# V of a pair of heads stored as head, 64 zeros, head: the products of attention weights and V over 128 columns

## The chip, the cores and the metric

The kernel runs on one core of a Trainium2 chip. Its time is the device time of one execution in microseconds (us); lower is better.

## What is computed

Two layers over a sequence of 512 tokens of width 1024, in fp32: a layer of stick-breaking attention with 16 heads of 64, a layer of a gated linear recurrence (HGRN2), each followed by a squared-ReLU MLP of width 4096. The change lies in the attention:

```python
for t0 in range(0, seq, 128):
    t1 = t0 + 128
    z = einsum('bhqd,bhkd->bhqk', q[:, :, t0:t1], k[:, :, :t1]) * scale
    causal = arange(t1)[None, :] < (t0 + arange(128))[:, None]
    log_stay = where(causal, log_sigmoid(-z), 0.0)
    log_between = cumsum(log_stay, axis=3, reverse=True) - log_stay
    weights = where(causal, exp(log_sigmoid(z) + log_between), 0.0)
    outs.append(einsum('bhqk,bhkd->bhqd', weights, v[:, :, :t1]))
```

The output of the heads goes through a projection (`sb_w_o`) and is added to the residual stream.

## The kernel before

The tokens are four blocks of 128 (`TT = 4`). Matrix products with weights run as three fp32r matmuls per step, on a high and a low part of each operand: the weights come as slabs of 256 or 512 columns, each in two halves of 512 KB. SyncE fetches a half into a raw buffer (tag `wr`, three buffers, line 257), ScalarE casts it to the high part (`wh`, line 266), VectorE subtracts to get the low part (`wl`, line 267). High and low parts have two buffers each, so the slab ahead is split as soon as TensorE has left the slab before. The first slab is written into two `wr` buffers by hand (line 1170) and split in four pieces at lines 540 and 541.

Attention (`attention`, line 501) goes over four groups of four heads. For a group it projects Q, K and V (`gemm_x`, 24 matmuls of 256 columns per block of tokens) and starts tasks for its two pairs of heads. `prepare_pair` (line 615) transposes K and Q of a pair (`pk`, `pq`). `head` (line 642) is one head: `z_of(T)` makes the scores of token block T and their sigmoids (`sn`, `sg`, lines 661 and 662), a scan and a product on VectorE (lines 664 and 668); `turn(T)` transposes the weights of block T, T + 1 transposes into `pa`, and brings them to SBUF as `at` (lines 682 and 683); `apply(T)` multiplies them with V:

```python
o = blk(shared["po"], T)[j * SB_DH : (j + 1) * SB_DH, :]
for b in range(T + 1):
    mm(o, vs[0][:, b, hc : hc + SB_DH], blk(at[T], b), b == 0, b == T)
```

V is the stationary operand (128 tokens by the 64 columns of one head), the weights are the moving one (128 columns), all fp32. Head j = 0 of a pair writes partitions 0 to 63 of the bank `po`, head j = 1 partitions 64 to 127. Per head these are 1 + 2 + 3 + 4 = 10 matmuls, 160 in all; the trace shows an fp32 matmul that is no transpose as two rows. When both heads are done, `split_out` (line 416) brings the bank to SBUF as `oh` and `ol`.

The order of TensorE's work is fixed by hand: `Line` counts an estimated time for each matmul and takes up the tasks by the delays in `LAG`, between the matmuls of the projections. So the pieces of a head stand among projection matmuls, and a run of `po` matmuls is followed by projections, by scores or by transposes. The order of the other engines' work is set by the scheduler of the language from priorities and its own estimate.

The tag `B` (two buffers) holds V of a group, later a part of the MLP's raw weights and V of the recurrence; line 607 writes V, scaled, on ScalarE. In the MLP a round is four slabs of `mlp_w1` (lines 844 to 862), and then seven half slabs made from `mlp_w2` (`Seven`), whose raw parts (`raw`, line 288) are fetched on the same queue of SyncE. Four rounds make one MLP, and there are two MLPs.

Of the kernel before, what the change touches and what calls it, by code (L numbers as in the profile page):

```python
# [8 lines left out]
F32 = mybir.dt.float32  # L9
# [3 lines left out]
AF = mybir.ActivationFunctionType  # L13
# [3 lines left out]
P = 128  # L17
D = 1024
S = 512
KT = D // P  # L20
TT = S // P
EPS = 1e-6
SLAB = 256
FF = 4 * D
SB_DH = 64
# [34 lines left out]
def trunk(  # L60
# [17 lines left out]
    nc = tc.nc  # L78
    PSUM = bass.MemoryType.PSUM
    cp = ctx.enter_context(tc.tile_pool(name="cp", bufs=1))  # L80
    wp = ctx.enter_context(tc.tile_pool(name="wp", bufs=2))
# [10 lines left out]
    def sb(tag, shape=(P, S), dt=F32, name=None):  # L92
        pool = gp if tag in "PQ" else ap
        return pool.tile(list(shape), dt, tag=tag, bufs=BUFS[tag], name=name or tag)
# [57 lines left out]
    def mm(o, lhsT, rhs, start, stop, **kw):  # L152
        n = rhs.shape[-1]
        nc.tensor.matmul(o, lhsT=lhsT, rhs=rhs, start=start, stop=stop, **kw)  # L154
        line.at += COST[rhs.dtype] * max(n, 64)
# [5 lines left out]
    def blk(t, n):  # L161
        return t[:, n * P : (n + 1) * P]
# [16 lines left out]
    def gain(layer, j, kt):  # L179
# [15 lines left out]
        out=later[:, 3 * P :], in_=later[:, 3 * P :], pattern=[[-1, P]], compare_op=ALU.is_gt,  # L195
# [4 lines left out]
        out=before[:, P:], in_=before[:, P:], pattern=[[1, P]], compare_op=ALU.is_gt,  # L200
# [49 lines left out]
    def slab_halves(spec):  # L250
        w, r0, kt, c0, nc_ = spec
        hi = wp.tile([P, kt, nc_], F32R, tag="wh", bufs=2, name="wh")
        lo = wp.tile([P, kt, nc_], F32R, tag="wl", bufs=2, name="wl")
        h = kt // 2

        def load(a):
            raw = wp.tile([P, h, nc_], F32, tag="wr", bufs=3, name="wr")
            r = r0 + a * h * P
            nc.sync.dma_start(
                out=raw, in_=w[r : r + h * P, c0 : c0 + nc_].rearrange("(k p) c -> p k c", p=P)  # L260
            )
            return raw

        def split(a, raw):
            c = slice(a * h, (a + 1) * h)
            nc.scalar.copy(hi[:, c, :], raw)  # L266
            nc.vector.tensor_tensor(out=lo[:, c, :], in0=raw, in1=f(hi[:, c, :]), op=ALU.subtract)  # L267

        return hi, lo, load, split

    def seven(w, r0):

        b = {}

        def rows(i, j, a):
            r = r0 + i * (D // 2) + a * 2 * P
            return w[r : r + 2 * P, j * S : (j + 1) * S].rearrange("(k p) c -> p k c", p=P)

        def load(i, j):

            tag = {(0, 0): "B", (1, 0): "X5", (0, 1): "R4", (1, 1): "R4"}[i, j]
            shape = (P, 10 * P) if tag == "X5" else (P, TT, SLAB)
            b[i, j] = []
            for a in range(2):
                t = sb(tag, shape, name="raw")
                t = t if tag == "X5" else t.rearrange("p t c -> p (t c)")
                t = t[:, : 2 * S].rearrange("p (k c) -> p k c", c=S)
                nc.sync.dma_start(out=t, in_=rows(i, j, a))
                b[i, j].append(t)

        def flip(at, plus):

            for a in range(2):
                nc.scalar.mul(b[at][a], b[at][a], -1.0)  # L294
                nc.gpsimd.dma_start(out=b[at][a], in_=plus(a), accum_op=ALU.add)

        def slab(at):
            hi = wp.tile([P, KT // 2, S], F32R, tag="wh", bufs=2, name="wh")
            lo = wp.tile([P, KT // 2, S], F32R, tag="wl", bufs=2, name="wl")
            for a in range(2):  # L300
                c = slice(2 * a, 2 * a + 2)
                nc.scalar.copy(hi[:, c, :], b[at][a])  # L302
                nc.vector.tensor_tensor(  # L303
                    out=lo[:, c, :], in0=b[at][a], in1=f(hi[:, c, :]), op=ALU.subtract
                )
            return hi, lo

        def early():
            load(0, 1)
            load(1, 1)  # L310

        def t1():
            flip((0, 1), lambda a: rows(0, 0, a))

        def slab_t1():
            got = slab((0, 1))
            for a in range(2):
                nc.gpsimd.dma_start(out=b[0, 1][a], in_=rows(1, 1, a), accum_op=ALU.add)  # L318
            flip((0, 0), lambda a: b[0, 1][a])
            return got  # L320

        def slab_b21():
            got = slab((1, 0))
            flip((1, 0), lambda a: b[0, 1][a])
            return got

        slabs = [
            lambda: slab((0, 0)), slab_t1, slab_b21, lambda: slab((1, 1)), lambda: slab((0, 1)),
            lambda: slab((0, 0)), lambda: slab((1, 0)),
        ]  # L330
        steps = (early, lambda: load(0, 0), lambda: load(1, 0), t1)
        return [("load", g) for g in steps], [("slab", g) for g in slabs]
# [168 lines left out]
    def attention(norm):  # L501
# [23 lines left out]
        wsl, raws = start["w"], start["raws"]  # L525
# [38 lines left out]
        for g in range(4):  # L564
            ss = sb("ss", (P, 2, 4 * TT), name="ss") if g else ss0
            qk = [] if g else [dst]
            for which in range(len(qk), 2):
                dst = sb("R4", (P, TT, SLAB), name="qk")
                qk.append(dst)
                wsl = weights.next()  # L570
                for hf in range(2):
                    p = ps("mm" if g else "tr")
                    for u in range(2):
                        yield from gemm_x(p[:, u * SLAB : (u + 1) * SLAB], wsl, 2 * hf + u, acts)
                    evac(p, 2 * hf, 2, which, dst, ss)
            m = sb("mqk", (P, 32), name="mqk")
            for which in range(2):
                nc.vector.scalar_tensor_tensor(
                    out=m[:, 16 * which : 16 * which + 16].rearrange("p (t h) -> p t h", h=4),
                    in0=ss[:, which, :].rearrange("p (t h) -> p t h", h=4), scalar=1.0 / SB_DH,  # L580
                    in1=em[:, :, None].to_broadcast([P, TT, 4]), op0=ALU.mult, op1=ALU.add,
                )
            rq = rsqrt(m, 32, "rq")
            q, k = qk
            for which in range(2):
                v = qk[which].rearrange("p t (h d) -> p (t h) d", d=SB_DH)
                nc.vector.tensor_tensor(
                    out=v, in0=v,
                    in1=rq[:, 16 * which : 16 * which + 16, None].to_broadcast([P, 16, SB_DH]),
                    op=ALU.mult,  # L590
                )
            vs = []
            for pair in range(2):
                shared = {"po": None}
                ready = line.spawn(prepare_pair(q, k, pair, shared))
                for j in range(2):
                    heads.append(line.spawn(head(ready, vs, pair, j, shared, outs, 2 * g + pair)))
            wsl = weights.next()
            V = sb("B", (P, TT, SLAB), name="V")
            for hf in range(2):  # L600
                p = ps("mm")
                for u in range(2):
                    yield from gemm_x(p[:, u * SLAB : (u + 1) * SLAB], wsl, 2 * hf + u, acts)
                for u in range(2):
                    t = 2 * hf + u
                    nc.scalar.activation(
                        out=V[:, t, :], in_=p[:, u * SLAB : (u + 1) * SLAB], func=AF.Copy,
                        scale=r[:, t : t + 1],
                    )
            vs.append(V)  # L610
        return outs, heads
# [30 lines left out]
    def head(ready, vs, pair, j, shared, outs, slot):  # L642
        yield [ready]
        yield max(0.01, shared["at"] + LAG["q"][j] - line.at)
        kst, qh, ql = shared["k"][j], shared["q"][j], shared["ql"][j]
        hc = (2 * pair + j) * SB_DH
        while live["sg"] >= BUFS["X5"]:
            yield 0.2
        live["sg"] += 1
# [35 lines left out]
        def apply(T):  # L685
            if shared["po"] is None:
                shared["po"] = ps("av", name="po")
            o = blk(shared["po"], T)[j * SB_DH : (j + 1) * SB_DH, :]
            for b in range(T + 1):
                mm(o, vs[0][:, b, hc : hc + SB_DH], blk(at[T], b), b == 0, b == T)  # L690

        for step in LAG["head"]:
            if isinstance(step, float):
                yield step
            else:
# [3 lines left out]
                {"z": z_of, "t": turn, "a": apply}[kind](T)  # L699
                if step == ("t", TT - 1):  # L700
                    live["sg"] -= 1
        if j == 1:
            outs[slot] = split_out(shared["po"])


# [173 lines left out]
    def hgrn(norm):  # L879
# [4 lines left out]
        for hp in range(4):  # L884
# [19 lines left out]
            for j in range(2):  # L904
# [14 lines left out]
                got[j] += [fr, kk]  # L919
                if j == 0:  # L920
                    task = line.spawn(take_turns(got, LAG["s0"]))
            V = sb("B", (P, TT, SLAB), name="Vh")
            G = sb("R4", (P, TT, SLAB), name="G")
            for n in range(2):
                wsl = weights.next()
# [228 lines left out]
    def trunk_steps():  # L1154
# [12 lines left out]
    w0, r0, _, c0, _ = weights.plan.pop(0)  # L1167
    start = {
        "w": [wp.tile([P, KT, SLAB], F32R, tag=t, bufs=2, name=t) for t in ("wh", "wl")],
        "raws": [wp.tile([P, KT // 2, SLAB], F32, tag="wr", bufs=3, name="wr") for _ in range(2)],  # L1170
    }
    for c in range(4):
        for j in range(2):
# [73 lines left out]
```

## Time and profile before

| | us |
|---|---|
| runs: lowest, median, highest | 1294.69, 1297.34, 1298.52 |
| the profiled execution | 1297.17 |
| its span | 1295.5 |
| TensorE busy in the span | 1259.6 (97%) |
| VectorE busy | 956.2 (74%) |
| ScalarE busy | 611.6 (47%) |
| GpSimd busy | 146.7 (11%) |

A busy time counts the time in which at least one instruction ran; matmuls overlap, so a busy TensorE need not be at its peak. For TensorE the distance between two starts says more than the length of a row. Rows of the timeline give start, length, engine, line, operation, tiles (out<-in), rows by columns of the stationary operand and shape of the moving one, and the number of merged instructions; an idle time ahead of a row stands in brackets, with what ended it.

### The profile page before, as it was taken

The numbers are of one execution on the slowest core, as the hardware profiler recorded it, in microseconds if no ns is written. First come the engines' busy times: TensorE is split into PE (matmuls) and PEld (weight loads), VectorE is DVE, ScalarE is ACT, GpSimd is POOL, SyncE is SP. The second block draws the span as 40 slices with busy tenths as digits, with TensorE's granted clock in tenths as the row PEclk, the third lists the DMA queues.
The fourth block names the chain that finished last, engine by engine and source line by source line (L and its number), as shares of the span: only waits on it lengthen the run. The fifth ranks groups of instructions, "written<-read, shape, count | busy, mean of one in ns | idle before, by whom it ended". The sixth has DMA issues, their size and how long they took to land. (4 is left out here: it accounts for less than half of the span.)

```text
span 1295.5 us, 17920 instructions
## 1 busy us (share of the span) xinstructions
PE 1259.6 (97%) x6817; PEld 1069.5 (83%) x6817; DVE 956.2 (74%) x1799; ACT 611.6 (47%) x991; POOL 146.7 (11%) x203
## 2 busy tenths in 40 slices
PE   7999999999999999999999999999999999999998
PEld 7989898778877878878878888888888788788787
DVE  4787688765676875867878888888666768667686
ACT  4555455534563634645552423333255536446362
POOL 1000001000020110100113131314000201002010
PEclk8999999999999999999999999999999999999999
DMA  6312124223285393671532222124521954827515
GB/s 185 106 33 66 34 66 130 83 89 90 66 179 178 72 237 114 125 212 54 97 98 66 65 66 72 59 85 137 170 69 62 215 164 84 246 74 172 169 31 133
DMA packets 104502, 144.23 MB, mean 111 GB/s; under 512 B 4856, under 2 KB 70560, under 8 KB 104416
## 3 DMA queue, kind: packets, MB, share of 16 engines
q1 hardware_dynamic: 91024, 109.22, 26.0%
q0 software_dynamic: 13392, 33.87, 14.8%
q8 instruction: 54, 0.88, 0.3%
q14 instruction: 32, 0.26, 0.1%
HBM read 124.19 MB, written 2.10 MB: 97 GB/s over the span
## 5 line engine op out<-in xcount | busy, mean ns | idle before, releaser
L154 PE MATMUL ps_mm<-xh,wh 128*128 128x512 f32 x592 | 232.6, 393 | 4.0 <-DVE xt L707 4.0
L154 PE MATMUL ps_mm<-xh,wl 128*128 128x512 f32 x592 | 230.5, 389 | 0.0
L154 PE MATMUL ps_mm<-xl,wh 128*128 128x512 f32 x592 | 230.5, 389 | 0.0
L266 ACT CAST wh<-wr 128x1024 fp32r<-128x1024 f32 x134 | 136.4, 1052 | 138.2 <-PE ps_mm L154 121.5
L267 DVE TENSOR_TENSOR wl<-wr,wh 128x1024 fp32r<-128x1024 f32 x134 | 163.2, 1232 | 17.1 <-ACT wh L266 17.0
L154 PE MATMUL ps_mm<-wh,xh 128*128 128x256 f32 x592 | 173.5, 293 | 0.0
L154 PE MATMUL ps_mm<-wl,xh 128*128 128x256 f32 x592 | 167.7, 283 | 2.7 <-DVE wl L541 2.7
L154 PE MATMUL ps_mm<-wh,xl 128*128 128x256 f32 x592 | 167.6, 283 | 0.0
L303 DVE TENSOR_TENSOR wl<-raw,wh 128x1024 fp32r<-128x1024 f32 x112 | 132.7, 1220 | 35.8 <-ACT wh L302 35.7
L154 PEld LDWEIGHTS ps_mm<-xh,wh 128*128 128x128 f32 x592 | 111.2, 188 | 28.7 <-issue 6.3
L302 ACT CAST wh<-raw 128x1024 fp32r<-128x1024 f32 x112 | 111.4, 1047 | 44.0 <-PE ps_mm L154 40.4
L154 PEld LDWEIGHTS ps_mm<-xh,wl 128*128 128x128 f32 x592 | 111.1, 188 | 23.3
L154 PEld LDWEIGHTS ps_mm<-xl,wh 128*128 128x128 f32 x592 | 111.2, 188 | 22.3
L707 DVE TENSOR_TENSOR xt<-xt,ps_mm 128x512 f32<-128x512 f32 x128 | 86.0, 682 | 47.9 <-PE ps_mm L154 47.7
L154 PEld LDWEIGHTS ps_mm<-wh,xh 128*128 128x128 f32 x592 | 113.4, 192 | 4.1 <-issue 3.6
L154 PEld LDWEIGHTS ps_mm<-wl,xh 128*128 128x128 f32 x592 | 113.5, 192 | 3.4 <-DVE wl L541 2.9
L154 PEld LDWEIGHTS ps_mm<-wh,xl 128*128 128x128 f32 x592 | 113.5, 192 | 0.0
L859 DVE SCALAR_TENSOR_TENSOR u<-ps_mm,R 128x512 f32<-128x512 f32 x60 | 41.4, 690 | 63.7 <-PE ps_mm L154 63.7
L318 POOL DMA_DIRECT2D raw<-in_mlp_w_dram x16 | 19.4, 1243 | 591.1 <-DVE wl L303 591.1
L294 ACT ACTIVATE raw<-raw 128x1024 f32<-128x1024 f32 x48 | 50.7, 1058 | 36.4 <-DMA raw<-in_mlp_w_dram 36.3
L664 DVE TENSOR_TENSOR_SCAN sn<-sn,later 128x128 f32<-128x128 f32 (+3 forms) x64 | 51.2, 816 | 8.1 <-ACT sn L661 7.1
L1021 DVE COPY_PREDICATED sc<-masks,ps_s 128x32 f32<-128x32 uint8 (+9 forms) x176 | 46.5, 298 | 13.0 <-PE ps_s L154 11.0
(235 smaller groups left out, 2538.9 us busy)
## 6 DMA issues: line engine op xcount, KB each, us to landing
raw<-in_mlp_w_dram SPq DMA_DIRECT2D x64, 512.0 KB, 6.3
wr<-in_mlp_w_dram SPq DMA_DIRECT2D x64, 512.0 KB, 4.5
raw<-in_mlp_w_dram POOLq DMA_DIRECT2D x32, 512.0 KB, 6.1
raw<-raw POOLq DMA_DIRECT2D x32, 512.0 KB, 6.1
wr<-in_hg_w_in_dram SPq DMA_DIRECT2D x32, 512.0 KB, 3.8
wr<-in_sb_w_qkv_dram SPq DMA_DIRECT2D x22, 512.0 KB, 3.7
wr<-in_sb_w_o_dram SPq DMA_DIRECT2D x8, 512.0 KB, 3.9
wr<-in_hg_w_o_dram SPq DMA_DIRECT2D x8, 512.0 KB, 4.0
```

What stands on the lines that cost most here:

```text
L154: nc.tensor.matmul(o, lhsT=lhsT, rhs=rhs, start=start, stop=stop, **kw)
L266: nc.scalar.copy(hi[:, c, :], raw)
L267: nc.vector.tensor_tensor(out=lo[:, c, :], in0=raw, in1=f(hi[:, c, :]), op=ALU.subtract)
L294: nc.scalar.mul(b[at][a], b[at][a], -1.0)
L302: nc.scalar.copy(hi[:, c, :], b[at][a])
L303: nc.vector.tensor_tensor(out=lo[:, c, :], in0=b[at][a], in1=f(hi[:, c, :]), op=ALU.subtract)
L318: nc.gpsimd.dma_start(out=b[0, 1][a], in_=rows(1, 1, a), accum_op=ALU.add)
L664: nc.vector.tensor_tensor_scan(out=rev, data0=rev, data1=later[:, S - W :][:, ::-1], initial=1.0, op0=ALU.mult, op1=ALU.max,)
L707: nc.vector.tensor_tensor(out=xt[h][:, t, :], in0=xt[h][:, t, :], in1=p, op=op)
L859: nc.vector.scalar_tensor_tensor(out=u, in0=p, scalar=0.0, in1=norm.R, op0=ALU.max, op1=ALU.mult)
L1021: nc.vector.copy_predicated(out=o, mask=mask.rearrange("p (g w) -> p g w", g=g)[:, None].to_broadcast([P, 2, g, w]), data=data.rearrange(" ...
```

## The change

V of a group becomes a tile of 128 x 4 x 2 x 192: for each token block and pair of heads first the 64 columns of head 0, then 64 zeros, then the 64 columns of head 1. GpSimd clears the middle (a new `memset` for each group, line 599 of the changed kernel), ScalarE writes the two heads in one instruction with a gap. The stationary operand of head 0 is columns 0 to 127 (head, zeros), that of head 1 columns 64 to 191 (zeros, head), so every product covers all 128 partitions of `po`, and both heads add into the same block; the first of the 20 matmuls of a pair starts the bank and the last one stops it. The bank is taken out by the head that comes last. V now needs half as much space again, so all users of tag `B` take tiles of 1536 elements, and the raw buffers `wr` become two instead of three.

```diff
-            raw = wp.tile([P, h, nc_], F32, tag="wr", bufs=3, name="wr")
+            raw = wp.tile([P, h, nc_], F32, tag="wr", bufs=2, name="wr")
...
-            shape = (P, 10 * P) if tag == "X5" else (P, TT, SLAB)
+            shape = (P, {"X5": 10 * P, "B": 12 * P, "R4": 8 * P}[tag])
...
-                shared = {"po": None}
+                shared = {"po": None, "n": 0}
...
-            V = sb("B", (P, TT, SLAB), name="V")
+            V = sb("B", (P, TT, 2, 3 * SB_DH), name="V")
+            nc.gpsimd.memset(V[:, :, :, SB_DH : 2 * SB_DH], 0.0)
...
+                    v = V[:, t].rearrange("p a (b d) -> p a b d", d=SB_DH)[:, :, 0::2, :]
                     nc.scalar.activation(
-                        out=V[:, t, :], in_=p[:, u * SLAB : (u + 1) * SLAB], func=AF.Copy,
-                        scale=r[:, t : t + 1],
+                        out=v, in_=p[:, u * SLAB : (u + 1) * SLAB].rearrange(
+                            "p (a b d) -> p a b d", b=2, d=SB_DH
+                        ),
+                        func=AF.Copy, scale=r[:, t : t + 1],
                     )
...
-            o = blk(shared["po"], T)[j * SB_DH : (j + 1) * SB_DH, :]
+
+            o = blk(shared["po"], T)
             for b in range(T + 1):
-                mm(o, vs[0][:, b, hc : hc + SB_DH], blk(at[T], b), b == 0, b == T)
+                shared["n"] += 1
+                mm(
+                    o, vs[0][:, b, pair, j * SB_DH : j * SB_DH + P], blk(at[T], b),
+                    shared["n"] == 1, shared["n"] == TT * (TT + 1),
+                )
...
-        if j == 1:
+        if shared["n"] == TT * (TT + 1):
             outs[slot] = split_out(shared["po"])
...
-            V = sb("B", (P, TT, SLAB), name="Vh")
+            V = sb("B", (P, 12 * P), name="Vh")[:, : 8 * P].rearrange("p (t c) -> p t c", c=SLAB)
...
-        "raws": [wp.tile([P, KT // 2, SLAB], F32, tag="wr", bufs=3, name="wr") for _ in range(2)],
+        "raws": [wp.tile([P, KT // 2, SLAB], F32, tag="wr", bufs=2, name="wr") for _ in range(2)],
```

TensorE, the second and third run of `po` of the first pair of heads, among projection matmuls (`ps_mm`) and transposes (`pa`); the numbers are columns of the output's partitions by columns moved:

```order
 L154 MATMUL ps_mm<-wh,xl 128x256
 L158 MATMUL pa<-ident,sg 128x128 x3
-L154 MATMUL po<-at,V 64x128 x2
+L154 MATMUL po<-at,V 128x128 x2
 L158 MATMUL pa<-ident,sg 128x128 x2
-L154 MATMUL po<-at,V 64x128
+L154 MATMUL po<-at,V 128x128
 L154 MATMUL ps_mm<-wh,xh 128x256
 L154 MATMUL ps_mm<-wl,xh 128x256
```

Nothing moved: on TensorE the whole program keeps its order, and only the width of the 160 products differs.

ScalarE at the start, from the last split of the first slab (line 540 before, 539 now) over the casts of the K slab (line 266) to the evacuation of the first Q projection. Before:

```order
L540 CAST wh<-wr 128x512
L266 CAST wh<-wr 128x1024 x2
L511 ACTIVATE sqq<-ps_mm 128x256
L517 COPY qk<-ps_mm 128x256
L511 ACTIVATE sqq<-ps_mm 128x256
L517 COPY qk<-ps_mm 128x256
L511 ACTIVATE sqq<-ps_z 128x256
```

Now:

```order
L539 CAST wh<-wr 128x512
L266 CAST wh<-wr 128x1024
L510 ACTIVATE sqq<-ps_mm 128x256
L516 COPY qk<-ps_mm 128x256
L510 ACTIVATE sqq<-ps_mm 128x256
L516 COPY qk<-ps_mm 128x256
L266 CAST wh<-wr 128x1024
L510 ACTIVATE sqq<-ps_z 128x256
```

The cast of the second half of the K slab went behind four evacuations.

The queue of SyncE at the border from the first to the second round of the first MLP: halves of `mlp_w1` slabs (`wr`) and the raw parts of `mlp_w2` of the round (`raw`). Before:

```order
L259 DMA wr_4073<-in_mlp_w1_dram 128x4x256
L259 DMA wr_4077<-in_mlp_w1_dram 128x4x256
L259 DMA wr_4115<-in_mlp_w1_dram 128x4x256
L288 DMA raw_4025<-in_mlp_w2_dram 128x2x512
L288 DMA raw_4027<-in_mlp_w2_dram 128x2x512
...
L288 DMA raw_4191<-in_mlp_w2_dram 128x2x512
L259 DMA wr_4119<-in_mlp_w1_dram 128x4x256
L259 DMA wr_4195<-in_mlp_w1_dram 128x4x256
```

Now:

```order
L259 DMA wr_4077<-in_mlp_w1_dram 128x4x256
L259 DMA wr_4081<-in_mlp_w1_dram 128x4x256
L287 DMA raw_4029<-in_mlp_w2_dram 128x2x512
L287 DMA raw_4031<-in_mlp_w2_dram 128x2x512
...
L287 DMA raw_4195<-in_mlp_w2_dram 128x2x512
L259 DMA wr_4119<-in_mlp_w1_dram 128x4x256
L259 DMA wr_4123<-in_mlp_w1_dram 128x4x256
L259 DMA wr_4199<-in_mlp_w1_dram 128x4x256
```

The first half of slab 1 of the next round (`wr_4115` before, `wr_4119` now) went from ahead of the eight `raw` fetches to behind them.

## Rows read from the trace of the kernel before

**Rows 1.** Attention: us, then PE, PEld, DVE, ACT, POOL busy, clock, DMA, GB/s.

```profile
47.00:290.00 243.00, 237.73 (x1695) 207.20 (x1694) 186.91 (x350) 122.33 (x260) 8.17 (x13) 0.99 0.24 73
```

**Rows 2.** TensorE's waits, 47 to 300 us: total us, times, longest.

```profile
PE z L154 <- ACT sg L662: 3.2, 3, 1.2
PE po L154 <- DVE at L683: 1.2, 2, 0.6
```

**Rows 3.** Timeline of TensorE, the first run of `po`: start, length in us.

```profile
70.69 0.38 PE L158 MATMUL pa<-ident,sg 128*128 128x128 f32 x2
71.00 0.43 PE L154 MATMUL po<-at,V 128*64 128x128 f32 x2
71.36 0.38 PE L154 MATMUL ps_mm<-wh,xh 128*128 128x256 f32 x1
71.58 0.28 PE L154 MATMUL ps_mm<-wl,xh 128*128 128x256 f32 x1
```

**Rows 4.** Timeline, VectorE and TensorE, a run between transposes.

```profile
76.80 0.59 DVE L683 TENSOR_TENSOR at<-pa,before 128x256 f32<-128x256 f32 x2
...
77.26 0.87 PE L154 MATMUL po<-at,V 128*64 128x128 f32 x6
...
78.06 0.55 PE L158 MATMUL pa<-ident,sg 128*128 128x128 f32 x3
```

**Rows 5.** Timeline of TensorE, the last run of `po`.

```profile
286.05 1.09 PE L154 MATMUL po<-at,V 128*64 128x128 f32 x8
287.07 0.50 PE L154 MATMUL ps_mm<-wh,oh 128*128 128x512 f32 x1
```

**Rows 6.** Timeline of TensorE, transposes of K and Q among projections.

```profile
59.26 0.28 PE L154 MATMUL ps_mm<-wh,xl 128*128 128x256 f32 x1
59.38 0.60 PE L158 MATMUL pk<-ident,qk 128*128 128x128 f32 x4
59.82 0.60 PE L158 MATMUL pq<-ident,qk 128*128 128x128 f32 x4
60.17 0.36 PE L154 MATMUL ps_mm<-wh,xh 128*128 128x256 f32 x1
60.38 0.28 PE L154 MATMUL ps_mm<-wl,xh 128*128 128x256 f32 x1
```

**Rows 7.** Timeline of TensorE, full-width fp32 products in the recurrence.

```profile
722.34 0.61 PE L154 MATMUL po_h<-Vh,sc 128*128 128x128 f32 x4
```

**Rows 8.** Groups of instructions by form: weight loads (busy us, mean ns).

```profile
L154 PEld LDWEIGHTS po<-at,V 128*64 128x64 f32 x320 | 33.3, 136 | 12.6 <-issue 7.1 <-DVE at L683 2.0 <-ACT sg L662 0.7
L154 PEld LDWEIGHTS po_h<-Vh,sc 128*128 128x128 f32 x64 | 9.4, 192 | 0.3
```

**Rows 9.** Timeline at the start: VectorE, the queue of SyncE, TensorE.

```profile
25.79 0.68 DVE L541 TENSOR_TENSOR wl<-wr,wh 128x512 fp32r<-128x512 f32 x1
...
26.50 0.37 SPq L259 DMA_DIRECT2D wr<-in_sb_w_qkv_dram  x1
...
31.28 0.28 PE L154 MATMUL ps_tr<-wl,xh 128*128 128x256 f32 x1
```

**Rows 10.** DMA issues: times, KB each, median us from issue to landing.

```profile
wr<-in_mlp_w_dram SPq DMA_DIRECT2D x64, 512.0 KB, 4.5
...
wr<-in_sb_w_qkv_dram SPq DMA_DIRECT2D x22, 512.0 KB, 3.7
```

**Rows 11.** Timeline of VectorE and ScalarE, border of rounds in the first MLP.

```profile
396.39 1.22 DVE L267 TENSOR_TENSOR wl<-wr,wh 128x1024 fp32r<-128x1024 f32 x1
...
398.13 1.22 DVE L267 TENSOR_TENSOR wl<-wr,wh 128x1024 fp32r<-128x1024 f32 x1
...
401.39 1.05 ACT L266 CAST wh<-wr 128x1024 fp32r<-128x1024 f32 x1 [2.57 <-DMA wr<-in_mlp_w_dram]
...
404.10 0.69 DVE L859 SCALAR_TENSOR_TENSOR u<-ps_mm,R 128x512 f32<-128x512 f32 x1 [0.40 <-PE ps_mm L154]
...
409.31 2.01 ACT L266 CAST wh<-wr 128x1024 fp32r<-128x1024 f32 x2 [3.42 <-PE ps_mm L154]
```

More of the change, by code (lines that the diff above doesn't have):

```diff
@@ L285, in load @@
                 t = sb(tag, shape, name="raw")
-                t = t if tag == "X5" else t.rearrange("p t c -> p (t c)")
                 t = t[:, : 2 * S].rearrange("p (k c) -> p k c", c=S)
@@ L645, in head @@
         kst, qh, ql = shared["k"][j], shared["q"][j], shared["ql"][j]
-        hc = (2 * pair + j) * SB_DH
         while live["sg"] >= BUFS["X5"]:
```

## The prediction

> **What bounds the kernel now.** I read the busy times by stretch first, because the change edits one stage: attention runs from about 47 to 290 us. There TensorE is busy 237.73 of 243 us, VectorE 186.91, ScalarE 122.33 and GpSimd 8.17 [rows 1]. So TensorE sets the pace of this stage, and what it no longer does is worth time, as long as VectorE (77% busy) keeps up. The list of TensorE's waits says the same from the other side: before 300 us the two largest are 3.2 us in 3 waits on the sigmoids of the scores and 1.2 us in 2 waits on the finished attention weights [rows 2]. Then I read TensorE's instructions in order of time around the products of weights and V (`po`), because busy time hides what lies between two pipelined matmuls; the number to read is the distance from one start to the next.
>
> The first run of `po` is one fp32 matmul, which the trace shows as two rows. Ahead of it stand two transposes at 70.69; they follow each other after 0.11, so the second starts at 70.80 and the first `po` row at 71.00, 0.20 later. From 71.00 to the next projection matmul are 0.36 us, and from that one to its successor 0.22 [rows 3]. In the last run eight rows need 1.02 us from the first of them to the start behind the run [rows 5]. A run between transposes takes 0.80 for six rows until the next transpose [rows 4]. Now the same kind of place without the 64-column shape: fp32 transposes over the full 128 columns. They start 0.12 after a projection matmul, follow each other at 0.11, the next projection matmul starts 0.35 after the first of four, and its successor 0.21 later [rows 6]. Three steps of 0.109 are 0.327 of that 0.35, so leaving a full-width group costs some 0.03, where leaving a `po` run costs 0.20. TensorE thus pays when it changes between the 64-column shape and the full one, at both ends of every run.
>
> **What the change does, part by part.**
>
> *The switch.* The order of TensorE's instructions stays; each of the 160 `po` matmuls becomes 128 columns wide. There are 64 runs, the first at 71.00 [rows 3], the last at 286.05 [rows 5]; 43 are followed by projections or scores and 21 by transposes. For one run that ends in projections, with its times from the rows: entering 0.20 instead of 0.11, saved 0.09; the first step inside is 0.16 instead of 0.11 (0.36 = 0.16 + 0.20 [rows 3]; 1.02 = 0.16 + 6 x 0.11 + 0.20 [rows 5]), saved 0.05; leaving 0.20 instead of 0.03, saved 0.17; the step behind it 0.22 instead of 0.21, saved 0.01. Together 0.32, times 43 is 13.8 us. For a run ahead of transposes: 0.09 + 0.05, then 0.20 to the transpose instead of 0.11, and the step after that again 0.16 instead of 0.11: 0.28, times 21 is 5.9 us. Sum 19.7. The steps inside may become a little longer: four full-width fp32 rows that are no transposes take 0.61 [rows 7] where four transposes take 0.60 [rows 6], so some 0.003 a step, 256 steps, 0.8 us. I take **19 us** off TensorE. From below, if only the way out were saved (the 43 x 0.17), it is 7 us; a loss is possible only by the weights, which is a rival below.
>
> *The wider weights.* A load of 64 columns takes 136 ns, a full-width fp32 load 192 [rows 8]. On 320 rows that is 320 x 56 ns = 17.9 us more of loading. I cost it at nothing, since loads run beside the matmul ahead: the rows of [rows 7] have 192 ns loads and still follow each other within 0.11. The Trainium skill, "TensorE: Matmul & The Clock Gate", section on LDWEIGHTS, has a load take its columns divided by 1.2 GHz, so by the page 53 ns more each and an estimate of 17 us: the rule speaks against the change, the trace has the same price but shows it covered, and by the rule alone almost all of the gain would be gone.
>
> *How much of the 19 us comes through.* The weights that `po` reads come from VectorE. The run at 77.26 starts while the two instructions that finish its weights run from 76.80 to 77.39 [rows 4]: here TensorE already stands at the edge. Three runs lie ahead of it in this burst, so about 1 us that they and its own entry save turns into a wait there. Bounds: if VectorE's work in the stage stays at 186.91 us against 243 - 19 = 224, it is 83% busy, and nothing need be lost; if in each of the eight pairs of heads one such edge takes back all that four runs save (4 x 0.31), 10 us are lost. I take half, **5 us**: the first pair of a group has its scores, transposes and weights packed close and the second has gaps.
>
> *One staging buffer less, at the start.* The raw halves of the weights now share two buffers instead of three, and the first slab holds both. So the second half of the K slab can only be fetched when the last split of the first slab ends, at 25.79 + 0.68 = 26.47; in the trace the queue issues its next fetch at 26.50 [rows 9]. It lands after 3.7 us [rows 10], at 30.2, is cast in 1.05 and split in 1.22 (durations of [rows 11]), so it is ready at 32.5. TensorE wants it for the fifth of eight steps of the K projection; that low half is first read at 31.28 [rows 9]. Cost **1.2 us**, from 0 (landing in 2.5 us) to 3. ScalarE's order is already bent round it: that cast now stands behind four evacuations.
>
> *The same buffer in the MLPs.* At the six borders between rounds the third buffer lets the first half of slab 1 arrive long ahead. Now it waits for the split that begins at 396.39 and ends at 397.61, the second half for the next, about 399.3. With a landing of 4.5 us [rows 10] the second half is there at 403.85, cast and split by 406.1, and the evacuation of the first product, which stands behind that split on VectorE, is done at 406.8 instead of 404.79. TensorE is on slab 0 until 409.31 [rows 11], and only then needs that bank and those weights. Cover 2.5 us, cost nothing; where a landing is longer than 7 us, all beyond it is paid six times. In the trace of before ScalarE waits 2.57 us at this border for the second half and nobody on TensorE notices.
>
> *The rest.* Four clears of the zero columns go to GpSimd; 13 instructions took it 8.17 us in this stage [rows 1], so some 0.6 each, on an engine that is idle for 235 us; the third clear waits for the first group's products, and behind it stand only clears for later heads. The evacuations of V write the same number of elements in two pieces. The order of ScalarE and VectorE changes by a few places within a pair (the cast of the finished pair comes ahead of two sigmoids); I cost it at nothing, plus or minus 2 us.
>
> Sum: -19 + 5 + 1.2 = **-12.8 us**. The profiled execution took 1297.17 us (1295.5 of span), which is 0.2 under the median 1297.34; so 1284.4 against that execution, and 1284.5 against the median.
>
> **The rivals.** *All comes through*: no edge takes anything back, -18, 1279. For it: few waits now, VectorE at 77%. Against it: the edge at 77.26. *Half of it comes back*: the edges take 10 us, -8, 1289.5. *No change*: the wider loads are not covered in a `po` run, because here the stationary operand is V and every row loads anew; -19 + 17.9 + 1.2 = 0, 1297. Against it [rows 7], the same fp32 shape with V in this kernel, though there V is the moving operand. It also covers the case in which the switch is not what costs the 0.20, so that the full shape keeps it. *Slower*: the two staging buffers. Place: second half of slab 1 at the six borders of rounds. To end 4 us above the median it must return the gain and more, 17 us, so 2.8 at each border: a landing of 7 + 2.8 = 9.8 us would do it, 1301.5. Against it the 4.5 us landing; for it that other transfers of the MLP run in the same stretches.
>
> **How the numbers follow.** A measurement of this kernel can tell about 0.3%, 3.9 us. Forecast with its own bounds, 0.60; all comes through, 0.12; half comes back, 0.15; no change, 0.08; slower, 0.05. The first three are faster by more than 3.9 us: 0.87. Range: down to 1276, where everything comes through and the granted clock, 0.99 in this stage [rows 1], comes to 1.00 (up to 2.4 us); up to 1292, where 10 us come back, the start costs 3 and another short fall of the clock comes in. That leaves out the two last cases.
>
> **What would show it.** Right: `po` rows of 128 columns, next projection 0.03 behind a run's last row, the first step 0.11; the attention stage 12 to 14 us shorter, with TensorE's waits on the weights and the sigmoids up by about 5. A wait of about 1 us at 31 us on the split of the K slab. Nothing at the MLP borders but a longer wait of ScalarE for the fetch. Wrong: `po` steps of 0.17 or more (the loads), a distance of 0.20 still standing behind runs (not the switch), TensorE waiting for weights at the round borders (the buffer), or VectorE above 90% in the stage.

## The result and the profile after

The changed kernel took **1283.69 us** (median of 3 runs, 1282.32 to 1284.05) against 1297.34: a ratio of 0.9890, 95% interval 0.9866 to 0.9913. That is 13.65 us less; 12.8 were forecast. On a second chip its ratio to the kernel before was 0.9912 (0.9899 to 0.9926). The profiled execution took 1282.32, its span 1280.6; against the 1295.5 of before that is 14.9 us less. Its mean granted clock is 0.996, the same as before.

Line numbers shift by a few in the changed kernel: the sigmoids are line 664, the attention weights 685, the projection's addition to the residual 714.

**The stage.** The work that stood between 47 and 290 us [rows 1] now ends 16 us earlier, so the same piece is 47 to 274 (columns as there: us, busy PE, PEld, DVE, ACT, POOL, clock, DMA share, GB/s):

```profile
47.00:274.00 227.00, 219.92 (x1696) 209.83 (x1695) 186.32 (x353) 121.43 (x260) 9.07 (x15) 0.99 0.26 79
```

TensorE has 1696 instructions as it had 1695, and VectorE 186.32 us of work as it had 186.91; only the stage is shorter. The granted clock is alike in both: 1.00 but for one short stretch at 0.50, the lower of TensorE's two levels (1.2 GHz), from 251 to 254 us before and from 240 to 243 now, each time behind two waits of about 0.9 and 1.0 us (in the second trace of the changed kernel, below, the same two waits stand with no such stretch). VectorE is now busy for 186.32 of 227 us, 82%, where the prediction had worked out 83%. Weight loads run for 209.83 us, 2.6 us more than before in a stage that is 16 us shorter; what hides them is tried below.

**The runs of `po`.** The timeline of TensorE at the first run and at the last one (start, length, us), which answer to [rows 3] and [rows 5]:

```profile
70.92 0.38 PE L158 MATMUL pa<-ident,sg 128*128 128x128 f32 x2
71.13 0.39 PE L154 MATMUL po<-at,V 128*128 128x128 f32 x2
71.28 0.36 PE L154 MATMUL ps_mm<-wh,xh 128*128 128x256 f32 x1
71.48 0.28 PE L154 MATMUL ps_mm<-wl,xh 128*128 128x256 f32 x1
...
270.38 1.05 PE L154 MATMUL po<-at,V 128*128 128x128 f32 x8
271.19 0.47 PE L154 MATMUL ps_mm<-wh,oh 128*128 128x512 f32 x1
```

From the first `po` row to the projection behind it were 0.36 us and are now 0.15: one step of 0.11 and 0.03 to leave. The eight rows of the last run took 1.02 us to the next start and now take 0.81, which is 7 x 0.11 and 0.03. From the start of the first run to the start of the last one it was 286.05 - 71.00 = 215.05 us; now it is 270.38 - 71.13 = 199.25. So **15.8 us** went between these two rows, and 0.2 more in the last run: all of the gain lies in this stage.

**What came back.** TensorE's waits from 47 to 300 us (total us, times, longest), to be read beside [rows 2]. The third of them was there before as well; its row of before comes first, then the three of now, then the run that stood at the edge in [rows 4]:

```profile
PE ps_mm L154 <- DVE xt L707: 1.0, 1, 1.0
```

```profile
PE z L154 <- ACT sg L664: 3.1, 3, 1.1
PE po L154 <- DVE at L685: 3.0, 6, 0.6
PE ps_mm L154 <- DVE xt L714: 1.0, 1, 1.0
```

```profile
77.67 0.49 PE L154 MATMUL po<-at,V 128*128 128x128 f32 x2 [0.61 <-DVE at L685]
78.00 0.49 PE L158 MATMUL pa<-ident,sg 128*128 128x128 f32 x3
```

The waits on the weights rose from 1.2 us in 2 to 3.0 in 6; the sigmoids and the one evacuation stay where they were. That is 7.1 us of idle time in place of 5.4, 1.7 more. Counted from start to start, the four runs that wait now and did not before (at 77.67, 92.09, 191.61 and 209.35 us) take 0.78, 0.33, 0.78 and 0.56 us longer at that step than before: **2.4 us** came back, where 5 were allowed.

**Outside the stage.** Three places, in the order of time: the start, a border of two rounds in the first MLP, and the border to the recurrence (first the timeline of TensorE; then of ScalarE and VectorE; then of ScalarE, with TensorE's waits from 630 to 660 us):

```profile
31.44 0.38 PE L154 MATMUL ps_tr<-wl,xh 128*128 128x256 f32 x1 [0.88 <-DVE wl L267]
```

```profile
388.15 1.05 ACT L266 CAST wh<-wr 128x1024 fp32r<-128x1024 f32 x1 [1.70 <-DMA wr<-in_mlp_w_dram]
...
390.38 0.69 DVE L866 SCALAR_TENSOR_TENSOR u<-ps_mm,R 128x512 f32<-128x512 f32 x1
...
393.34 2.01 ACT L266 CAST wh<-wr 128x1024 fp32r<-128x1024 f32 x2 [1.17 <-PE ps_mm L154]
```

```profile
637.41 1.05 ACT L266 CAST wh<-wr 128x1024 fp32r<-128x1024 f32 x1 [0.30 <-DMA wr<-in_hg_w_in_dram]
```

```profile
PE ps_x L158 <- DVE xl L435: 2.0, 2, 1.3
```

At the start TensorE waits 0.88 us for the second half of the K slab, as forecast; from start to start it falls back by 1.1 us between 30 and 48 us (from 0.9 ahead of the kernel before to 0.2 behind it). At the round border the evacuation ends at 390.38 + 0.69 = 391.07 and TensorE leaves slab 0 at 393.34, 16 us earlier than at the same place of before [rows 11]: 2.3 us to spare, and TensorE does not wait. At the border to the recurrence ScalarE's cast waits 0.30 us for a fetch, which it did not do before; the evacuations of the transposes stand behind that cast, and TensorE's wait for them is 2.0 us, where the kernel before had 1.2 in the same stretch (645 to 675 us there):

```profile
PE ps_x L158 <- DVE xl L436: 1.2, 2, 0.6
```

So 0.8 us were lost at a place that the prediction had not looked at. The price of this place is not fixed. In the second trace of the changed kernel (run again, below) TensorE waits longer there, and the granted clock then lies at the lower level, where the first trace has 1.00 (the waits from 630 to 660 us, and a stretch with the columns of the stage's row):

```profile
PE ps_x L158 <- DVE xl L435: 3.3, 2, 2.4
```

```profile
640.00:646.00 6.00, 5.06 (x16) 4.28 (x17) 4.33 (x12) 2.02 (x4) 0.00 (x0) 0.50 0.27 87
```

In that execution 3.5 us went at this border against the kernel before. From start to start, the step with the longer of the two waits is 0.98 us in the three traces with three staging buffers, and 1.5 to 2.8 us in the ten with two.

Sum over the span: -16.0 in the stage, +1.1 at the start, +0.8 at the recurrence, +0.2 in the second MLP, and -0.9 because the first transfers (blocks of `x`, the gain of K) landed that much earlier in this execution, which is chance: the row that stands at 31.16 us before stands at 32.82 and 29.75 in two experiments with the same start. That is -14.8, and the span shows -14.9.

### The profile page after: what moved, and what is told of

It reads as the page before. It is cut to its first block, busy times and chain, and to the rows that moved or that the text cites. A ratio compares the mean times of both kernels' runs of the same rounds, so it can differ in the third digit from the quotient of the medians.

```text
span 1280.6 us, 17916 instructions
## 1 busy us (share of the span) xinstructions
PE 1241.3 (97%) x6817; PEld 1071.3 (84%) x6817; DVE 955.4 (75%) x1799; ACT 611.1 (48%) x991; POOL 148.4 (12%) x207
## 3 DMA queue, kind: packets, MB, share of 16 engines
q0 software_dynamic: 13392, 33.87, 14.9%
## 5 line engine op out<-in xcount | busy, mean ns | idle before, releaser
L154 PE MATMUL ps_mm<-wl,s31h 128*128 128x512 f32 x128 | 51.2, 400 | 4.1 <-DVE wl L302 4.1
```

## The experiments

Two theories on the gain were to be told apart (the 64-column shape costs at every change of shape, or something else in the change brings the time), and one question on the loss: do the two staging buffers, or the order of VectorE, make the new waits? Each ratio below is to runs of the kernel before beside it on the same chip, with medians of 1295.58, 1295.81 or 1295.68 us; it can differ a little from the quotient of two medians. Differences in us are worked out from the ratio and 1297.34.

**The width alone.** The kernel before with 128 columns of V and nothing else: no zeros, three staging buffers.

```diff
...
-            o = blk(shared["po"], T)[j * SB_DH : (j + 1) * SB_DH, :]
+            o = blk(shared["po"], T)
...
-                mm(o, vs[0][:, b, hc : hc + SB_DH], blk(at[T], b), b == 0, b == T)
+                mm(o, vs[0][:, b, pair * P : (pair + 1) * P], blk(at[T], b), b == 0, b == T)
```

> The kernel before, in which only the width of the product changes: the stationary operand is the 128 columns of both heads of the pair as V lies before (no zeros, no memset, three staging buffers, the starts and stops of before), so the two heads overwrite each other and the output is not the reference's. Theory (the 64-column shape costs TensorE a change at both ends of every run): the whole gain and a little more, since the staging buffer stays: attention 16 us shorter, no wait at 31 us, 15.5 to 18 us under the kernel before, 1279 to 1282. Rival (the gain comes from the single accumulation of both heads, the later bank or the new order of VectorE): within 4 us of before.

Measured: 1280.78 us, ratio 0.9875 (0.9859 to 0.9890), so 16.2 us (14.3 to 18.3) below the kernel before. Its waits in the stage, 47 to 300 us:

```profile
PE z L154 <- ACT sg L661: 3.1, 3, 1.1
PE po L154 <- DVE at L682: 3.0, 6, 0.6
PE ps_mm L154 <- DVE xt L706: 1.4, 2, 1.0
```

The width carries the whole gain. (Its stage is 1.0 us shorter than the changed kernel's, but the granted clock is 1.00 all through it; the second trace of the changed kernel has 1.00 and the same length.) The waits on the weights are the same 3.0 us in 6 as in the changed kernel, with three staging buffers and the old order on ScalarE and VectorE. So they are the refill: TensorE has become faster than what feeds it. The wait at the start and the longer one at the recurrence are absent here (1.2 us in the latter stretch, as before).

**Two buffers alone.** The kernel before with `bufs=2` for `wr` in both places.

> The kernel before with two staging buffers instead of three and nothing else. Theory (what the traces of before and after show as the price of the buffer: a wait of 1.04 us at 31 us and 0.7 us more at the border from the first MLP to the recurrence): 1 to 2.5 us slower than before, about 1299. Rival A (the buffer costs at the borders of MLP rounds, hidden in the change by its gain): 4 us and more. Rival B (it costs nothing): within 0.5 us.

Measured: 1299.35 us, ratio 1.0025 (1.0016 to 1.0034), so 3.2 us more (2.1 to 4.4), between the theory and its first rival. Its timeline has both waits of the changed kernel, TensorE's at the start and ScalarE's at the recurrence:

```profile
31.08 0.39 PE L154 MATMUL ps_tr<-wl,xh 128*128 128x256 f32 x1 [0.86 <-DVE wl L267]
```

```profile
654.64 1.05 ACT L266 CAST wh<-wr 128x1024 fp32r<-128x1024 f32 x1 [0.37 <-DMA wr<-in_hg_w_in_dram]
```

From start to start they cost 1.1 and 0.8 us, and the borders of MLP rounds add nothing. Of the rest, 0.9 us stands at 385 us and 0.5 at 555, where TensorE waits for the weights made from `mlp_w2`. Whether the buffer causes these is open. At the first place the wait is 0.1 to 0.3 us in the three traces with three buffers and 0.0 to 1.1 in the ten with two; at the second it is 0.4 to 0.8 and 0.3 to 0.8. A shift of the same kind, 1.2 us, also stands in the second MLP of the width alone, which has three buffers.

**More runs, narrow and wide.** If the price is paid for each change of shape, more runs must cost, and with the full width they must not. The products of token blocks 2 and 3 (three and four matmuls) are cut into two runs, with one step of the projections between them where one is left: 92 runs in place of 64.

```diff
-            main = Task(gen)
+            main = self.main = Task(gen)
...
-        def apply(T):
+        def apply(T, blocks=None):
...
-            for b in range(T + 1):
+            for b in blocks or range(T + 1):
...
-                {"z": z_of, "t": turn, "a": apply}[kind](T)
+                if kind == "a" and T > 1:
+                    apply(T, range(2))
+                    if line.main.ready(line.at) and not line.main.done:
+                        line.main.step(line.now)
+                    apply(T, range(2, T + 1))
+                else:
+                    {"z": z_of, "t": turn, "a": apply}[kind](T)
```

In the kernel before (64 columns):

> The kernel before with the product of token blocks 2 and 3 cut in two by one step of the projection (three matmuls of 256 columns, taken from where they stood before): 92 runs of 64-column products instead of 64, the same 6817 rows of TensorE. Theory (0.33 us for each run: 0.09 in, 0.05 after the first step, 0.17 out, 0.02 behind): 28 x 0.33 = 9 us slower than before, 1305 to 1308. Rival (the cost is per product, of the 64-column shape itself, or of the first run of a burst only): within 2 us of before.

In the changed kernel (128 columns):

> The changed kernel with the same cut: 92 runs of 128-column products instead of 64. Theory (no change of shape, no price of a run): within 1.5 us of the changed kernel, 1282 to 1285. Rival (any cut between fp32 and fp32r products costs, and the width only hides it): about 9 us slower than the changed kernel, 1293.

Measured: 1306.28 us in the kernel before, ratio 1.0077 (1.0064 to 1.0091), so 10.0 us (8.3 to 11.8) for 28 more runs, **0.36 us a run** (0.30 to 0.42). In the changed kernel 1282.4 us, ratio 0.9899 (0.9885 to 0.9914) against 0.9890 without the cut: no difference. The same piece in both traces, the first two blocks of a cut product, narrow and then wide (TensorE's timeline):

```profile
75.85 0.65 PE L154 MATMUL po<-at,V 128*64 128x128 f32 x4
76.43 0.39 PE L154 MATMUL ps_mm<-wh,xh 128*128 128x256 f32 x1
76.65 0.28 PE L154 MATMUL ps_mm<-wl,xh 128*128 128x256 f32 x1
```

```profile
76.44 0.61 PE L154 MATMUL po<-at,V 128*128 128x128 f32 x4
76.81 0.36 PE L154 MATMUL ps_mm<-wh,xh 128*128 128x256 f32 x1
77.01 0.28 PE L154 MATMUL ps_mm<-wl,xh 128*128 128x256 f32 x1
```

Four narrow rows hold TensorE for 0.58 us until the projection, four wide ones for 0.37, and the entry costs its 0.09 besides. This settles that the change of shape is the cost.

**How near are the loads?** The prediction took the wider loads as covered. Here each product moves two halves of 64 columns, with a load of the same 128 columns of V for each: twice the loads, the same columns moved.

```diff
-                mm(
-                    o, vs[0][:, b, pair, j * SB_DH : j * SB_DH + P], blk(at[T], b),
-                    shared["n"] == 1, shared["n"] == TT * (TT + 1),
-                )
+                for c in range(2):
+                    u = slice(c * P // 2, (c + 1) * P // 2)
+                    mm(
+                        o[:, u], vs[0][:, b, pair, j * SB_DH : j * SB_DH + P], blk(at[T], b)[:, u],
+                        shared["n"] == 1 and c == 0, shared["n"] == TT * (TT + 1) and c == 1,
+                    )
```

> The changed kernel with each of the 160 products cut into two that move 64 columns of weights each, so 640 rows and 640 full-width weight loads instead of 320. The columns moved stay the same, only the loads double. Theory 1, the loads are only just covered by a step of 0.112 us: a row of half the moving columns still takes about 0.11, the 320 rows more cost 320 x 0.11 = 35 us, 1319 us, PE's starts inside a run 0.11 apart. Theory 2, the loads are well covered (a load costs at most half a step): rows follow at 0.056, time as the changed kernel, 1284 plus or minus 3. In between, the distance inside a run is the true price of a load. The prediction took the loads as hidden without saying by how much; theory 1 would mean that the cover was bare.

Measured: 1311.42 us, ratio 1.0111 (1.0093 to 1.0129), 22 per mille or some 28.7 us above the changed kernel. The first run in its timeline:

```profile
71.45 0.38 PE L158 MATMUL pa<-ident,sg 128*128 128x128 f32 x2
71.67 0.56 PE L154 MATMUL po<-at,V 128*128 128x64 f32 x4
72.03 0.36 PE L154 MATMUL ps_mm<-wh,xh 128*128 128x256 f32 x1
```

Four rows of half the columns take 0.36 us to the next start, and two of the full columns took 0.15 (71.13 to 71.28). Row by row the first step of a run is 0.058 (its load ran beside the transposes), and the 512 later ones have a median of 0.112. So theory 1 is nearly right: a full-width fp32 load needs 0.112 us of its own, which is what a step with 128 moving columns lasts (0.111 for the first step in the changed kernel, whose load ran beside the transposes as well). The cover of the wider loads was complete but bare. The Trainium skill, "TensorE: Matmul & The Clock Gate", section on LDWEIGHTS, gives columns divided by 1.2 GHz, an estimate of 0.107 us for 128; the 0.112 of this run lies near it. The prediction's sentence on that rule added the load to the step; here the longer of the two is what counts, and with 128 moving columns they are equal.

**Can the refill be had back?** With the switch gone it costs nothing to move runs, so the products were put some 0.7 us, by the order's own count, later behind their transposes, by the delays in `LAG`.

```diff
-        ("z", 0), 0.46, ("z", 1), 2.26, ("z", 2), 1.2, ("t", 0), ("z", 3), 1.5, ("t", 1), ("a", 0),
-        1.54, ("t", 2), ("a", 1), 1.58, ("t", 3), ("a", 2), 1.37, ("a", 3),
+        ("z", 0), 0.46, ("z", 1), 2.26, ("z", 2), 1.2, ("t", 0), ("z", 3), 1.5, ("t", 1), 0.7, ("a", 0),
+        0.84, ("t", 2), 0.7, ("a", 1), 0.88, ("t", 3), 0.7, ("a", 2), 0.67, ("a", 3),
```

> The changed kernel with the products of weights and V put about one projection step later after the transposes that make their weights (the delays ahead of them; the sum of the delays of a head is the same but for 0.0 to 0.1). Theory (the 3.0 us in 6 waits of the products on the attention weights are what is left of the refill, and an idle switch makes it free to move runs): these waits go, TensorE's waits on the instruction that makes the weights fall from 3.0 to under 0.5 us and the time by 2 to 3 us, to about 1281, ratio 0.987. Rival: the order of the stage shifts as a whole, and waits on scores' sigmoids or on the projections' evacuations take their place: 1284 to 1288, waits in the stage as large as before or larger.

Measured: 1285.67 us, ratio 0.9918 (0.9905 to 0.9931), no better. Its waits from 47 to 300 us:

```profile
PE ps_mm L154 <- DVE xt L714: 4.3, 1, 4.3
PE z L154 <- ACT sg L664: 3.9, 4, 1.2
PE pa L158 <- DVE at L685: 0.8, 1, 0.8
PE po L154 <- DVE at L685: 0.5, 1, 0.5
```

The waits on the weights fell from 3.0 to 0.5 us, and others took 4.9 us in their place (4.3 for 1.0, 3.9 for 3.1, 0.8 for none): the rival. The large one is a projection that waits for a bank which VectorE empties late. The next run keeps the old delays for the last group of heads, whose work stands around that projection.

> As the run with the later products, but only for the heads of the first three groups; the last group keeps the delays of the changed kernel. In the run with all groups the waits on the attention weights fell from 3.0 to 0.5 us as expected, and a single wait of 4.3 us at 231 us, of a projection of the output on VectorE, ate it. Theory (that wait comes from the last group's heads being late, since the projection of the output stands among them): it is gone, and what the first groups save, about 2 us, is left: 1281.5 us, ratio 0.9875. Rival (the first groups' shift already makes it): the long wait stays, 1285.

Measured: 1284.28 us, ratio 0.9913 (0.9899 to 0.9927); the changed kernel itself, on the same chip, 1284.23 (below). This theory fell. The projection and the instructions of VectorE ahead of it, from its timeline:

```profile
231.64 0.39 PE L158 MATMUL z<-kst,qh 128*128 128x256 f32 x1 [0.60 <-ACT sg L668]
...
236.41 0.79 PE L158 MATMUL ps_mm<-wh,oh 128*128 128x512 f32 x1 [4.26 <-DVE xt L718]
```

```profile
232.84 0.96 DVE L670 TENSOR_TENSOR_SCAN sn<-sn,later 128x384 f32<-128x384 f32 x1
233.72 0.74 DVE L674 TENSOR_TENSOR sg<-sg,sn 128x127 f32<-128x127 f32 x2
234.49 0.42 DVE L646 CAST qh<-qh 64x512 fp32r<-64x512 f32 x1
234.95 0.69 DVE L670 TENSOR_TENSOR_SCAN sn<-sn,later 128x256 f32<-128x256 f32 x1
235.67 0.69 DVE L718 TENSOR_TENSOR xt<-xt,ps_mm 128x512 f32<-128x512 f32 x1
```

VectorE has no gap here; the emptying of the bank (line 718) stands behind the scores of the last pair. So the delays of the first three groups alone are enough for it. Moving TensorE's runs moves the waits, it does not remove them: at such places VectorE is the bound, though it is idle for 18% of the stage.

**A third place at the start.** The second half of the K slab is fetched into a buffer of the tag `X5`, which is free until the first scores.

```diff
+    made = []
+
...
+        made.append(spec)
+
         def load(a):
-            raw = wp.tile([P, h, nc_], F32, tag="wr", bufs=2, name="wr")
+            if a and len(made) == 1:
+                raw = sb("X5", (P, 10 * P), name="wr")[:, : h * nc_]
+                raw = raw.rearrange("p (k c) -> p k c", c=nc_)
+            else:
+                raw = wp.tile([P, h, nc_], F32, tag="wr", bufs=2, name="wr")
```

> The changed kernel with the second half of the K slab at the start fetched into a free buffer of another tag instead of waiting for one of the two staging buffers. TensorE's order is the same. Theory (the wait of 0.9 us at 31.4 us comes from the staging buffer alone): the wait is gone, everything behind it 1.0 us earlier, 1282.7 us, ratio 0.9885. Rival: something else holds TensorE there or a little later (the attention stage begins with work that waits for VectorE), and less than 0.3 us is left of it at 60 us: 1283.7.

Measured: 1281.96 us, ratio 0.9896 (0.9880 to 0.9913), which can't be told from the changed kernel's 0.9890. In the trace TensorE no longer waits between 25 and 47 us, and it is 2.0 us ahead of the changed kernel's first trace from 42 to 232 us (0.9 of it because the first transfers landed earlier). The stage gives it 1.0 more, since its granted clock is 1.00 throughout; then 0.8 go in the first MLP and 1.7 at the border to the recurrence, where TensorE waits 1.5 us and its granted clock is 0.53 for a short stretch (columns as in the stage's row):

```profile
640.00:642.00 2.00, 2.00 (x9) 1.66 (x8) 1.15 (x4) 0.55 (x2) 0.00 (x0) 0.53 0.38 133
```

0.53 lies next to 0.5, the lower of the two levels; the changed kernel has 1.00 there in its first trace, and falls as well in its second. So the wait was the buffer's, as the theory said, and one us of it is less than this kernel's other differences from run to run. The two edits together, with the delays of all groups and then of the first three:

> Both edits together, the later products and the free buffer at the start. If both theories hold, 3 to 4 us below the changed kernel: about 1280, ratio 0.9865, faster than both kernels. If only the buffer helps, 1282.7. If the order of the later products makes waits of its own, 1283 to 1287.

Measured: 1284.16 us, ratio 0.9908 (0.9892 to 0.9925).

> The same with the free buffer at the start as well. Theory: 1 us below the run without it, some 3 us below the changed kernel: 1280.5 us, ratio 0.987, faster than both kernels; a fall of TensorE's granted clock can hide a us of it. Rival as for the run without the buffer: 1284.

> The changed kernel as it is, on the chip of the two runs above, to compare them with it directly: ratio 0.989 as before, 1283 to 1284 us.

Measured: 1283.25 us for the first, ratio 0.9903 (0.9890 to 0.9917), and 1284.23 for the changed kernel beside it, 0.9912 (0.9899 to 0.9926). The start is worth about a us here as expected, but the intervals overlap, and the theories that both edits together give 3 us or more fell. No version beats the changed kernel by more than about a us.

## Why the prediction was right, step by step

- *The switch, 19 us.* The stage became 16.0 us shorter although 2.4 us came back in it, so TensorE gave up 18.4. The working by parts held as well: over the 64 runs the medians now are 0.11 into a run (0.20 before), 0.111 for the first step inside (0.16), 0.03 out to projections and scores and 0.112 out to transposes (0.20), and 0.112 for the later steps (0.109). The runs with more pieces confirm the price by another way, 0.36 us a run against the 0.32 taken.
- *The wider weights, nothing.* Right, shown by the width alone. The reason was right but the cover was bare: the loads need 0.112 us each, as much as the step that hides them.
- *The refill, 5 us of 0 to 10.* The mechanism was right, down to the run at 77 us that now waits 0.61. The term was oversized: 2.4 us. So the stage shrank by 16 us, more than the 12 to 14 that were named as the sign, and TensorE's idle time rose by 1.7 us and not by about 5. The refill comes from the width alone, since the waits on the weights are the same with three buffers and the old order on VectorE.
- *The start, 1.2 us.* Measured 1.1, of which 0.9 is a wait at the instruction named; the wait goes with a third place for the fetch.
- *The borders of MLP rounds, nothing.* Right: 2.3 us to spare where 2.5 were worked out, with the second half cast at 388.15, against 403.85 less the 16 us, 387.9.
- *What the sum lacked.* The two buffers also act at the border to the recurrence, 0.8 us in the first trace and 3.5 with the clock's fall in the second; the step looked at the borders of MLP rounds only, though all slabs share the tag. The buffers alone cost 3.2 us (2.1 to 4.4) where the sum had 1.2; 1.4 us of that, in the first MLP, have no settled cause.
- *The rest, 0 plus or minus 2.* The moved order of ScalarE and VectorE left no trace: the waits of the stage are those of the width alone to within 0.4 us.

The refill was overestimated by 2.6 and the buffers underestimated by some 2, so it is partly luck that the sum came out nearer than its parts: -12.8 against -13.65.

Of the rivals, "all comes through" was nearest to the runs of the width alone; "no change" fell because the loads are covered; with fewer moving columns the loads do set the pace, as the run with halves shows. "Slower" needed a landing of 9.8 us at the borders, and the cast at 388.15 shows one as expected.

## What to carry to other kernels

Where narrow products stand in short runs among full-width ones, read the start-to-start distances at both ends of a run before counting columns: here the change of shape cost 0.3 us a run, three times a product's step, and zeros in the stationary operand removed it for nothing but memory. Check the memory that pays for it at every user of the buffer that gives way, not only at the one in mind. And where the padded operand loads anew for each product, compare the load with the step that covers it: in this kernel's fp32 products, 128 columns on both sides break even, and with 64 moving columns the loads set the pace.

## What the runs showed of the hardware that was not expected

- The cost of the shape is not only at the borders: the first step inside a run of 64-column products was 0.16 us, all later ones 0.109, in 63 of the 64 runs, whichever half of the partitions they wrote (the other one fell into the stretch at the lower clock). The Trainium skill, "TensorEngine Tiling (Array Packing)", Tiling Modes, has a change of the tiling mode drain TensorE; the runs with more pieces agree that the change costs, 0.36 us for going in and out.
- A step of 64 columns of output and 128 moving ones (0.109 us) was no faster than one of 128 (0.112): alone in its rows, the narrow product had no advantage to lose.
- A load of 128 columns that shows 192 ns in the trace lets the next one follow after 112 ns (medians of the run with halves), so the length of a load's row says little about its rate.
